# Letting transpositions and retention scores join TensorE's queue when their operands are estimated ready, in an fp32 two-block network

## The chip, the cores and the metric

One core of a Trainium2 chip runs the whole program once. The metric is the device time of one execution in microseconds; the time before is the median of three executions. A further execution was profiled, and every duration below comes from its trace.

## What is computed

256 tokens of width 2048 pass through two blocks, all in fp32 accuracy. Block 1 normalizes and modulates the tokens, mixes them, and runs a swiglu FFN of inner width 5632. Block 2 has its own mixer (attention, gated linear attention and a short convolution, merged by sigmoid gates) and a second FFN. What the change touches, cut from the reference:

```python
def token_mixer(h, ...):
    q, k, v, g_ret, u, gate_r, gate_s = jnp.split(h @ w_in, IN_SPLITS, axis=-1)
    q = rope(q, cos, sin)
    k = rope(k, cos, sin) * (RET_QK_DIM ** -0.5)
    ret = head_group_norm(retention(q, k, v))       # scores = q k^T * decay; 8 heads
    y_ret = (jax.nn.silu(g_ret) * ret) @ w_ret_out
    y_ssm = jax.nn.gelu(s5_ssm(u, ...))
    glu_a, glu_b = jnp.split(y_ssm @ w_s5_glu, 2, axis=-1)
    y_s5 = glu_a * jax.nn.sigmoid(glu_b)
    merged = jax.nn.sigmoid(gate_r) * y_ret + jax.nn.sigmoid(gate_s) * y_s5
    return merged @ w_out

def swiglu_ffn(h, w_ffn_in, w_ffn_out):
    a, b = jnp.split(h @ w_ffn_in, 2, axis=-1)
    return (jax.nn.silu(a) * b) @ w_ffn_out
```

## The kernel before

**Weights and items.** Every weight is used once. They come in units of 1 MB from `ws` into `raw` (four buffers, queue of SyncE). A unit holds two items of 128 rows x 1024 columns. For each item ScalarE copies `raw` into `whi` in a rounded format, VectorE subtracts to get `wlo`, and TensorE forms hi·hi, hi·lo and lo·hi: twelve matmuls of 128x512 per item (`gemm_tok`, `mm3`). Items are prepared up to four ahead (`AHEAD`, five buffers each of `whi` and `wlo`). Activations are kept as pairs of pages too (`h2h` and `h2l`, `ysh` and `ysl`, `xrh` and `xrl`). In between stand 96 modulation steps on VectorE, which multiply a whole `raw` by `cact`.

**Side tasks.** The rest is written as Python generators: `untok` (L446, turns token-major pages by TensorE transpositions against `ident` into a bank `sdb` and splits them), `retention` (L864), `gated` (L913), S5 and others. They yield the kind of engine that comes next and a delay: "P", "A", "V", or "W" for no condition. While the program is built, a planner keeps an estimated clock for each engine (`Engine`, `Times`). After each item `pump` steps the head task of each kind that `can` go on; "P" goes on if its time `t[2]` is no later than TensorE's clock plus `EARLY` = -0.25 us. For a new task, `t[2]` is that of its first yield:

```python
            t[3], wait = next(t[0])
            t[2] = max(self.times.mark, self.PE.clock if wait else 0.0) + wait
```

For `yield "P", 0.0` ahead of any instruction of the task itself, `mark` and `wait` are 0, so `t[2]` is 0: a task that starts with it goes on after the item that started it. `sd` yields "W" until one of three spare PSUM banks is estimated free. `finish` steps all tasks until a given one has ended. What is emitted is a fixed order on each engine; the planner does not exist on the chip.

**Who starts the tasks.** `gate_up` (FFN) multiplies the two banks of a stage into `fst` on VectorE and starts `untok` on them: 11 stages in each of two FFNs. `glu_a` multiplies the banks into `sg`, then by a gate page `gl`, adds `merged`, and starts `untok`: four times. `br_done` does the same with `sig` for the merge of block 2: four times. `ready` starts `retention(hp)` for a pair of heads when its q, k and v exist; q and k come from `rope_page` (two products and a sum on VectorE). `g_done(hp)` starts `gated(hp)`, which multiplies the retention output into `tg` and transposes it to `xr`, the input of the `w_ret_out` GEMM. Its four column groups of eight items each read `xr` through `xrf`; `ret_before(0)` first finishes all four `gated` tasks. S5 runs as a task beside all this, in four slabs of state; each fetches its inputs by many small DMAs and ends in the pages `ysh` and `ysl` of the glu stage.

All instructions show L150 in the profile, since `Engine` records each operation there; so they are told apart by the names of their tiles.

Of the kernel before, what the change touches and what calls it, by code (L numbers as in the profile page):

```python
# [24 lines left out]
EARLY = -0.25  # L25
# [128 lines left out]
class Core:  # L154
# [52 lines left out]
    def sd(self, n):  # L207
        while sum(self.times.free((f"bank{i}", 0)) <= self.PE.clock + BANK for i in self.sd_ids) < n:
            yield "W", 0.0
        self.sd_ids.sort(key=lambda i: self.times.free((f"bank{i}", 0)))  # L210
        return [self.sd_bank() for _ in range(n)]

    def sd_free(self, *banks):
        self.sd_ids.extend(self.sd_of.pop(b.tensor.name) for b in banks)
# [231 lines left out]
    def untok(self, pages, ident, dst, n, name):  # L446


        yield "P", 0.0
        for half in range(2):  # L450
            b, = yield from self.sd(1)
            for vb in range(2):
                for t in range(2):
                    at = 256 * half + 128 * vb
                    self.PE.transpose(b[:, 256 * vb + 128 * t:256 * vb + 128 * t + 128], pages[t][:, at:at + 128], ident)
            yield "A", 0.0
            dst[2 * n + half] = self.split_page(b, name)
            self.later.append(lambda b=b: self.sd_free(b))
            yield "P", 0.0
# [166 lines left out]
def program(K):  # L626
# [3 lines left out]
    G = {}  # L630
# [233 lines left out]
    def retention(hp):  # L864
        decs = [K.page("dec"), K.page("dec")]
        for par in range(2):
            K.S.dma_start(decs[par][:, :384], ins["decay"][:, 2 * hp + par, :])
        yield "P", 4.0
        q, k, v = qk["q", hp], qk["k", hp], vv.pop(hp)
        R = ret[hp] = [K.page("ret"), K.page("ret")]  # L870
        st = K.small.tile([128, 4, 6], F32, name="st", tag="st", bufs=2)
        mv = K.small.tile([128, 4, 2], F32, name="mv", tag="mv", bufs=2)
        rs = K.small.tile([128, 4], F32, name="rs", tag="rs", bufs=2)
        outs = []
        for par in range(2):
            rows = slice(64 * par, 64 * par + 64)
            dec = decs[par]
            s, = yield from K.sd(1)
            for j, i0, o0 in ((0, 0, 0), (1, 128, 256)):
                for half in range(2):  # L880
                    b = 256 * half
                    PE.matmul(s[:, o0:o0 + 256 - i0], k[rows, b + 128 * j:b + 128 * j + 128], q[rows, b + i0:b + 256],
                              start=half == 0, stop=half == 1)
            yield "V", 0.0
            sp = K.page("sp")
            V.tensor_mul(sp[:, :384], s[:, :384], dec[:, :384])
            K.sd_free(s)
            yield "P", 0.0
            o, = yield from K.sd(1)
            vs = slice(256 * par, 256 * par + 256)  # L890
            PE.matmul(o[:, :256], sp[:, 0:128], v[0][:, vs], start=True, stop=True)
            PE.matmul(o[:, 256:], sp[:, 128:256], v[0][:, vs], start=True, stop=False)
            PE.matmul(o[:, 256:], sp[:, 256:384], v[1][:, vs], start=False, stop=True)
            yield "V", 0.0
            for t in range(2):
                V.bn_stats(st[:, 2 * par + t, :], o[:, 256 * t:256 * t + 256])
                V.bn_aggr(mv[:, 2 * par + t, :], st[:, 2 * par + t, :])
            outs.append(o)
            yield "A", 0.0
        A.activation(rs, mv[:, :, 1], AF.Sqrt, bias=K.eps5)  # L900
        yield "V", 0.0
        V.reciprocal(rs, rs)
        for par in range(2):
            for t in range(2):
                n = 2 * par + t
                V.tensor_scalar(R[t][:, 256 * par:256 * par + 256], outs[par][:, 256 * t:256 * t + 256],
                                mv[:, n, 0:1], rs[:, n:n + 1], op0=OP.subtract, op1=OP.mult)
            yield "V", 0.0
        K.sd_free(*outs)

    xr = {}

    def gated(hp, tg):  # L913
        R = ret.pop(hp)
        for t in range(2):
            V.tensor_mul(tg[t], tg[t], R[t])
        yield "P", 0.0
        for par in range(2):
            b, = yield from K.sd(1)
            for vb in range(2):  # L920
                for t in range(2):
                    PE.transpose(b[:, 256 * vb + 128 * t:256 * vb + 128 * t + 128],
                                 tg[t][:, 256 * par + 128 * vb:256 * par + 128 * vb + 128], ident)
            yield "A", 0.0
            xr[2 * hp + par] = K.split_page(b, "xr")
            K.later.append(lambda b=b: K.sd_free(b))
            yield "P", 0.0
# [210 lines left out]
    def ready(it, src):  # L1138

        what, i = it  # L1140
        if what == "u":
            t = K.page("up")
            ut = t.rearrange("p (n t c) -> p n t c", n=2, t=4)
            uc = src[0].rearrange("p (n c t) -> p n t c", n=2, t=4)
            for n in range(2):
                A.activation(ut[:, n], uc[:, n], AF.Copy)
                K.G.dma_start(ub[2 * i + n], t[:, 256 * n:256 * n + 256])
        elif what == "v":
            vv[i] = [K.page("v"), K.page("v")]
            for p, ps in zip(vv[i], src):  # L1150
                A.activation(p, ps, AF.Copy)
        elif what in "rs":
            gate_done("rs".index(what), i)(0, src)
        else:
            qk[it] = rope_page(src[0], "qk")
        have.add(it)
        if what == "u" and all(("u", n) in have for n in range(4)):
            G["s5"] = K.start("s5", s5_run())
        for hp in range(4):
            if ("ret", hp) not in G and all((w, hp) in have for w in "qkv"):  # L1160
                G["ret", hp] = K.start("ret", retention(hp))
# [131 lines left out]
    def gate_load(n):  # L1293
        if n < 16 and n not in gl:
            gl[n] = K.page("gl")
            K.S.dma_start(gl[n], gsp[n])

    def ret_before(n):
        def f():
            if n == 0:  # L1300
                for hp in range(4):
                    K.finish(G["gt", hp])
                gate_load(0)
                gate_load(1)
            gate_load(2 * n + 2)
            gate_load(2 * n + 3)
        return f

    def ret_done(n):
# [2 lines left out]
                m = merged[n, t] = gl.pop(2 * n + t)  # L1312
                V.tensor_mul(m, ps, m)
        return f
    xrf = lambda k: K.halves_of(xr)(k)
    for n in range(4):
        K.gemm_tok([("w_ret_out", 512 * n)], xrf, ret_done(n), before=ret_before(n))

# [597 lines left out]
def plan():  # L1916
    K = Core()
    program(K)
    K.run()
    return K.units  # L1920
# [79 lines left out]
def trace(ctx, tc, ins, out, lives=None):  # L2000
    K = Core(tc, ins, out, ctx, lives)
    ctx.enter_context(tc.manual_schedule())
    program(K)
    K.run()
    return K
# [23 lines left out]
```

## Time and profile before

| | |
|---|---|
| median of three executions | 3358.95 us (3358.52 to 3359.52) |
| profiled execution | 3354.24 us, its span 3352.1 us |
| TensorE matmul (PE) busy | 3289.2 us, 98% |
| TensorE weight load (PEld) | 2773.6 us, 83% |
| VectorE (DVE) | 1994.5 us, 59% |
| ScalarE (ACT) | 1541.8 us, 46% |
| DMA | 737.62 MB, mean 220 GB/s |

Busy time is a share of the span. Matmuls are pipelined and their ends are modelled, so consecutive matmuls overlap in the rows; the distance between two starts is measured. The time that a row of the timeline has in brackets is the idle time of its engine ahead of it, with what released it. `PEclk` is the TensorE clock that was granted, as a share of full speed.

### The profile page before, as it was taken

Reading aid. Unit: us, or ns where it says so; the run is one execution under the profiler, and the core shown is the slowest. Engines: PE = TensorE matmul, PEld = TensorE weight load, DVE = VectorE, ACT = ScalarE, POOL = GpSimd, SP = SyncE. Lnnn points to the kernel's source line nnn. Section 1 sums busy time; section 2 is a strip of 40 time slices with the busy share of each in tenths; the row PEclk is TensorE's granted clock in tenths of the full one; section 3 lists DMA queues with packets and bytes.
Section 4 is the critical chain, followed back from the end, with each engine's and each line's share of the span. In section 5 each row is a group of like instructions: output and inputs, shape, how many; then the busy total and the mean of one; then the engine's idle time right before and its main releaser. Section 6 shows DMA issues by size and latency. Waiting matters only on the chain.

```text
span 3352.1 us, 42924 instructions
## 1 busy us (share of the span) xinstructions
PE 3289.2 (98%) x17276; PEld 2773.6 (83%) x17276; DVE 1994.5 (59%) x2192; ACT 1541.8 (46%) x1852; POOL 196.8 (6%) x311
## 2 busy tenths in 40 slices
PE   8999999999999999999999999999999999999999
PEld 7988888777888888888888999888778888888887
DVE  7987889777755565445545455455554544444444
ACT  5555555434644444444455444444434544444443
POOL 4611321100000000000000000000000000000000
PEclk9999999999999999999999999999999999999999
DMA  9976778777666666555555444555456455555653
GB/s 342 339 290 249 252 287 270 284 282 275 265 222 224 226 237 213 211 209 198 210 189 182 168 181 168 206 188 196 181 180 222 177 187 188 182 184 187 221 202 129
DMA packets 120489, 737.62 MB, mean 220 GB/s; under 512 B 15633, under 2 KB 19233, under 8 KB 36193
## 3 DMA queue, kind: packets, MB, share of 16 engines
q1 hardware_dynamic: 111778, 719.33, 59.1%
q0 software_dynamic: 7936, 14.50, 1.4%
q8 instruction: 135, 2.21, 0.3%
q10 hardware_dynamic: 576, 1.05, 0.1%
q14 instruction: 64, 0.52, 0.0%
HBM read 719.47 MB, written 14.70 MB: 219 GB/s over the span
## 4 chain that ended last, share of the span: by engine, by line
PE 89%; DVE 5%; DMA 3%; ACT 1%; issue 1%; SPq 0%; DVEq 0%; ACTq 0%
PE mmb L150 85%; PE sdb L150 4%; DMA raw<-ws 2%; DVE raw L150 1%; DVE wlo L150 1%; DVE fst L150 1%; ACT whi L150 1%; DVE sg L150 0%; ACT part L150 0%; DVE part L150 0%; DMA s5b<-s5bc 0%; DVE sig L150 0%; DVE t L150 0%; DVE u L150 0%; DVE xl L150 0%
## 5 line engine op out<-in xcount | busy, mean ns | idle before, releaser
L150 DVE TENSOR_TENSOR wlo<-raw,whi 128x1024 fp32r<-128x1024 f32 x1124 | 1365.6, 1224 | 1035.7 <-ACT whi L150 1034.4
L150 ACT ACTIVATE whi<-raw 128x1024 fp32r<-128x1024 f32 x1124 | 1183.7, 1059 | 1521.7 <-PE mmb L150 1355.8
L150 PE MATMUL mmb<-whi,hh 128*128 128x512 f32 x1169 | 463.1, 396 | 8.8 <-ACT part L150 4.5
L150 PE MATMUL mmb<-wlo,hh 128*128 128x512 f32 x1169 | 457.7, 392 | 2.8 <-DVE wlo L150 2.8
L150 PE MATMUL mmb<-whi,hl 128*128 128x512 f32 x1169 | 457.2, 391 | 0.0
L150 PE MATMUL mmb<-whi,h2h 128*128 128x512 f32 x704 | 276.5, 393 | 0.7 <-ACT h2h L150 0.7
L150 PE MATMUL mmb<-whi,h4h 128*128 128x512 f32 x704 | 276.5, 393 | 0.1
L150 PE MATMUL mmb<-whi,h4l 128*128 128x512 f32 x704 | 274.1, 389 | 0.4 <-DVE h4l L150 0.4
L150 PE MATMUL mmb<-wlo,h4h 128*128 128x512 f32 x704 | 274.3, 390 | 0.0
L150 PE MATMUL mmb<-wlo,h2h 128*128 128x512 f32 x704 | 274.3, 390 | 0.0
L150 PE MATMUL mmb<-whi,h2l 128*128 128x512 f32 x704 | 274.2, 389 | 0.0
L150 PEld LDWEIGHTS mmb<-whi,hh 128*128 128x128 f32 x1169 | 220.6, 189 | 56.7 <-ACT part L150 5.2
L150 PEld LDWEIGHTS mmb<-wlo,hh 128*128 128x128 f32 x1169 | 220.6, 189 | 51.5 <-DVE wlo L150 5.2
L150 PEld LDWEIGHTS mmb<-whi,hl 128*128 128x128 f32 x1169 | 220.7, 189 | 44.4
L150 DVE SCALAR_TENSOR_TENSOR raw<-raw,cact 128x2048 f32<-128x2048 f32 x96 | 219.5, 2286 | 17.2 <-DMA raw<-ws 16.7
L150 PE MATMUL mmb<-whi,h3h 128*128 128x512 f32 x576 | 227.5, 395 | 0.0
L150 PE MATMUL mmb<-whi,h3l 128*128 128x512 f32 x576 | 225.6, 392 | 0.0
L150 PE MATMUL mmb<-wlo,h3h 128*128 128x512 f32 x576 | 225.6, 392 | 0.0
L150 PE MATMUL mmb<-h3h,whi 128*128 128x256 f32 x784 | 225.4, 287 | 0.1
L150 PE MATMUL mmb<-h3l,whi 128*128 128x256 f32 x784 | 221.9, 283 | 0.6 <-DVE h3l L150 0.6
L150 PE MATMUL mmb<-h3h,wlo 128*128 128x256 f32 x784 | 221.8, 283 | 0.0
L150 PEld LDWEIGHTS mmb<-wlo,h4h 128*128 128x128 f32 x704 | 132.1, 188 | 27.8
(332 smaller groups left out, 4784.7 us busy)
## 6 DMA issues: line engine op xcount, KB each, us to landing
raw<-ws SPq DMA_DIRECT2D x657, 1024.0 KB, 4.9
gsp<-gate POOLq DMA_DIRECT2D x16, 256.0 KB, 6.3
gl<-gsp SPq DMA_DIRECT2D x16, 256.0 KB, 7.4
xl<-x1d SPq DMA_DIRECT2D x16, 256.0 KB, 5.3
x<-xT SPq DMA_DIRECT2D x8, 256.0 KB, 5.6
xl<-xt SPq DMA_DIRECT2D x8, 256.0 KB, 8.7
gb<-grow SPq DMA_DIRECT2D x8, 256.0 KB, 6.5
x1d<-u POOLq DMA_DIRECT2D x8, 256.0 KB, 3.5
```

The source lines that it names most:

```text
L150: return f(*args, **kw)
```

## The change

A new method `made` yields "W" for as long as the planner estimates that the operands named are not ready by TensorE's clock plus `EARLY`. `untok` calls it on its pages ahead of its first transposition, `retention` on q, k and the decay pages ahead of its first scores. `ret_before(0)` no longer finishes the gated tasks; `xrf(k)` finishes one when its pages are asked for and missing.

```diff
+    def made(self, *aps):
+        while self.PE.clock + EARLY < self.times.start(0.0, "", [], aps):
+            yield "W", 0.0
...
         yield "P", 0.0
+        yield from self.made(*pages)
         for half in range(2):
...
         yield "P", 4.0
         q, k, v = qk["q", hp], qk["k", hp], vv.pop(hp)
+        yield from K.made(q, k, decs[0], decs[1])
...
             if n == 0:
-                for hp in range(4):
-                    K.finish(G["gt", hp])
                 gate_load(0)
                 gate_load(1)
...
-    xrf = lambda k: K.halves_of(xr)(k)
+    def xrf(k):
+        if k // 2 not in xr:
+            K.finish(G["gt", k // 4])
+        return K.halves_of(xr)(k)
```

All engines have the same instructions as before, in another order. On TensorE, at the end of an FFN stage of block 1 (`mmb` are accumulators, `fst` the gated pages of that stage, `h2h` and `h2l` the FFN's input), before:

```order
L150 MATMUL mmb_8088<-whi_8354,h2h_8360 128x512
L150 MATMUL mmb_8088<-whi_8354,h2l_8361 128x512
L150 MATMUL mmb_8088<-wlo_8355,h2h_8360 128x512
L150 MATMUL sdb_8461<-ident_92,fst_8455 128x128
L150 MATMUL sdb_8461<-ident_92,fst_8456 128x128
...
L150 MATMUL mmb_8476<-whi_8385,h2h_8035 128x512
```

and with the change:

```order
L150 MATMUL mmb_8088<-wlo_8355,h2h_8360 128x512
L150 MATMUL mmb_8471<-whi_8385,h2h_8035 128x512
L150 MATMUL mmb_8471<-whi_8385,h2l_8036 128x512
L150 MATMUL mmb_8471<-wlo_8386,h2h_8035 128x512
L150 MATMUL mmb_8472<-whi_8385,h2h_8035 128x512
L150 MATMUL mmb_8472<-whi_8385,h2l_8036 128x512
L150 MATMUL mmb_8472<-wlo_8386,h2h_8035 128x512
...
L150 MATMUL sdb_8485<-ident_92,fst_8455 128x128
L150 MATMUL sdb_8485<-ident_92,fst_8456 128x128
...
L150 MATMUL mmb_8471<-whi_8405,h2h_8056 128x512
```

The first group of four transpositions stands one item (twelve matmuls, of which six are shown) further back, behind the first item of the next stage. The `sig` group moves in the same way, by one item.

On TensorE, at the end of a glu column group (`ysh` and `ysl` are the S5 output, `sg` the merged page), before:

```order
L150 MATMUL mmb_6681<-whi_6654,ysh_6378 128x512
L150 MATMUL mmb_6681<-whi_6654,ysl_6379 128x512
L150 MATMUL mmb_6681<-wlo_6655,ysh_6378 128x512
L150 MATMUL sdb_6754<-ident_92,sg_6670 128x128
L150 MATMUL sdb_6754<-ident_92,sg_6671 128x128
...
L150 MATMUL mmb_6769<-whi_6674,ysh_4077 128x512
```

and with the change:

```order
L150 MATMUL mmb_6681<-wlo_6655,ysh_6260 128x512
L150 MATMUL mmb_6764<-whi_6674,ysh_4131 128x512
...
L150 MATMUL mmb_6764<-whi_6694,ysh_4944 128x512
...
L150 MATMUL mmb_6765<-wlo_6695,ysh_4944 128x512
L150 MATMUL sdb_6794<-ident_92,sg_6670 128x128
L150 MATMUL sdb_6794<-ident_92,sg_6671 128x128
...
L150 MATMUL mmb_6764<-whi_6717,ysh_5629 128x512
```

Here two items (`whi_6674` and `whi_6694`, 24 matmuls) now stand between the last matmul of the group and its transpositions.

On TensorE, ahead of the `w_ret_out` GEMM (`tg` is the gated retention output, `u4` and `m1r` are S5's, `xrh` is the GEMM's input), before:

```order
L150 MATMUL mmb_5581<-wlo_5654,hh_1986 128x512
L150 MATMUL sdb_5834<-ident_92,tg_5811 128x128
L150 MATMUL sdb_5834<-ident_92,tg_5812 128x128
...
L150 MATMUL sdb_5845<-u4_5084,m1r_5488 64x64 x16
L150 MATMUL sdb_5846<-u4_5084,m1i_5489 64x64 x16
L150 MATMUL sdb_5879<-ident_92,tg_5811 128x128
L150 MATMUL sdb_5879<-ident_92,tg_5812 128x128
...
L150 MATMUL mmb_5900<-whi_5673,xrh_5166 128x512
```

and with the change:

```order
L150 MATMUL mmb_5895<-whi_5787,xrh_5176 128x512
...
L150 MATMUL sdb_5949<-u4_5043,m3_5510 64x64
L150 MATMUL sdb_5998<-ident_92,tg_5873 128x128
L150 MATMUL sdb_5998<-ident_92,tg_5874 128x128
...
L150 MATMUL mmb_5895<-whi_5857,xrh_5512 128x512
...
L150 MATMUL sdb_6042<-ident_92,tg_5873 128x128
L150 MATMUL sdb_6042<-ident_92,tg_5874 128x128
...
L150 MATMUL mmb_5895<-whi_5884,xrh_5760 128x512
```

The two groups of the last head pair stand behind the third and fourth item of the GEMM, not ahead of it, and no S5 products are placed between them by force. The first retention scores move back by 30 matmuls, into the first column group of a gate GEMM.

## Rows read from the trace of the kernel before

**Rows 1.** Waits of TensorE: who waits <- for whom: us in total, times, longest

```profile
PE sdb L150 <- DVE sg L150: 12.5, 8, 2.2
PE sdb L150 <- DVE fst L150: 9.2, 24, 0.8
PE sdb L150 <- DVE sig L150: 6.7, 8, 1.5
...
PE sdb L150 <- DVE qk L150: 2.7, 1, 2.7
PE sdb L150 <- DVE xrl L150: 2.4, 1, 2.4
PE sdb L150 <- DVE tg L150: 1.7, 2, 1.5
```

**Rows 2.** Timeline, TensorE and VectorE in FFN stages: start, us, engine, instruction

```profile
945.05 0.39 PE L150 MATMUL mmb<-wlo,h2h 128*128 128x512 f32 x1
...
947.18 0.48 PE L150 MATMUL mmb<-whi,h2h 128*128 128x512 f32 x1
...
1036.18 1.37 DVE L150 TENSOR_TENSOR fst<-mmb,fst 128x512 f32<-128x512 f32 x2 [2.67 <-PE mmb L150]
...
1036.43 0.39 PE L150 MATMUL mmb<-wlo,h2h 128*128 128x512 f32 x1
...
1037.91 0.48 PE L150 MATMUL mmb<-whi,h2h 128*128 128x512 f32 x1
...
1040.52 0.40 PE L150 MATMUL mmb<-wlo,h2h 128*128 128x512 f32 x1
...
1041.11 0.48 PE L150 MATMUL mmb<-whi,h2h 128*128 128x512 f32 x1
```

**Rows 3.** Timeline at the end of a glu column group, TensorE and VectorE

```profile
713.03 0.39 PE L150 MATMUL mmb<-wlo,ysh 128*128 128x512 f32 x1
...
714.07 2.74 DVE L150 TENSOR_TENSOR sg<-sg,gl 128x512 f32<-128x512 f32 x4
...
717.16 0.48 PE L150 MATMUL mmb<-whi,ysh 128*128 128x512 f32 x1
```

**Rows 4.** Timeline at the end of a merge column group of block 2, TensorE

```profile
2392.51 0.39 PE L150 MATMUL mmb<-wlo,xah 128*128 128x512 f32 x1
...
2395.19 0.48 PE L150 MATMUL mmb<-whi,h3h 128*128 128x512 f32 x1
```

**Rows 5.** Windows: us, busy PE PEld DVE ACT POOL, PEclk, DMA share, GB/s

```profile
294.90:298.40 3.50, 3.50 (x10) 2.69 (x10) 3.47 (x5) 0.00 (x0) 0.00 (x0) 0.51 0.52 176
...
2469.10:2472.60 3.50, 3.50 (x10) 2.61 (x10) 1.57 (x2) 0.25 (x1) 0.00 (x0) 0.51 0.69 250
500.00:520.00 20.00, 20.00 (x144) 16.55 (x143) 15.92 (x20) 11.02 (x13) 8.67 (x18) 1.00 0.86 158
680.00:700.00 20.00, 20.00 (x90) 16.57 (x89) 15.82 (x17) 7.69 (x8) 0.00 (x0) 1.00 0.99 385
700.00:820.00 120.00, 107.48 (x457) 86.89 (x456) 82.79 (x93) 46.70 (x52) 0.00 (x0) 0.94 0.70 255
```

**Rows 6.** Timeline around the first retention scores, TensorE and VectorE

```profile
288.71 1.29 DVE L150 TENSOR_TENSOR t<-s5x,s5b 128x512 f32<-128x512 f32 x2 [4.91 <-DMA s5b<-s5bc]
...
290.10 0.28 PE L150 MATMUL mmb<-hh,wlo 128*128 128x256 f32 x1
...
294.12 1.28 DVE L150 TENSOR_TENSOR rt<-mmb,rope 128x512 f32<-128x512 f32 x2
```

**Rows 7.** Timeline (ScalarE, TensorE) and one piece of the chain of waits

```profile
825.81 2.01 ACT L150 ACTIVATE whi<-raw 128x1024 fp32r<-128x1024 f32 x2 [8.47 <-DMA raw<-ws]
...
542.82 0.50 PE L150 MATMUL mmb<-wlo,hh 128*128 128x512 f32 x1 [0.58 <-DVE wlo L150]
...
506.66 15.99 DMA raw<-ws
```

**Rows 8.** Costliest groups of the page: busy us, mean ns | idle before

```profile
L150 DVE SCALAR_TENSOR_TENSOR raw<-raw,cact 128x2048 f32<-128x2048 f32 x96 | 219.5, 2286 | 17.2 <-DMA raw<-ws 16.7
```

## The prediction

> **What bounds the kernel now.** I read the table of the profile first: TensorE is busy 98% of a span of 3352.1 us, VectorE 59%, ScalarE 46%, so the end is set by TensorE's own list of matmuls and by what interrupts it. Next the waits of TensorE, grouped by who releases them [rows 1]. The reader should see that the named waits for `sg`, `fst`, `sig`, `qk`, `xrl` and `tg` are transpositions and retention scores (into the spare banks `sdb`) whose VectorE operands were still being made. They add up to 12.5 + 9.2 + 6.7 + 2.7 + 2.4 + 1.7 = 35.2 us. These are the places that the change edits.
>
> The ends of matmuls are modelled, so I take starts. In the FFN [rows 2] the last matmul of a stage starts at 1036.43 and the first of the next at 1037.91: 1.48 us, with four transpositions between them. One item later the same four transpositions, with their operands ready, fit between 1040.52 and 1041.11: 0.59 us. So a task's first group loses 1.48 - 0.59 = 0.89 us, its second nothing. The first task of each FFN takes 2.13 us (945.05 to 947.18) and loses 1.54. In the glu stage [rows 3] the first group spans 713.03 to 717.16: 4.13, a loss of 3.54. In the merge of block 2 [rows 4] 2392.51 to 2395.19: 2.68, a loss of 2.09.
>
> Last the granted clock by stretches [rows 5]: right after the wait for `qk`, each of the four for `sg` and two of the four for `sig`, TensorE is granted 0.51 for 3.5 us (seven such stretches; first and last stand there). That is the lower of its two levels, 1.2 instead of 2.4 GHz, nearly throughout, and loses 0.49 x 3.5 = 1.7 us each.
>
> **The change, part by part.** No instruction is added or removed on any engine; only their order differs. `made` costs nothing on the chip: it decides while the program is built. About ten DMA issues on SP's queue (decay and S5 loads among weights) and one group of S5 gathers on GpSimd's change places by a few; they are priced below with S5.
>
> *FFN transpositions.* There are 5632/512 = 11 tasks in each of two FFNs. Their first group goes behind one more item, twelve matmuls at 0.22 us (90 of them in 20.00 us, [rows 5]), 2.7 us. Are the operands there by then? VectorE's two products end at 1036.18 + 1.37 = 1037.55 [rows 2]; the transpositions would now start at 1036.43 + 0.23 + 2.7 = 1039.4. Margin 1.8 us. Removed: 20 x 0.89 + 2 x 1.54 = 20.9 us. The pages made from them are read in the down-projection, after all tasks; the last one moves into its first items, long before its own columns are due. What is late next: the ScalarE copy and VectorE subtraction of the transposed page, one item later, with nobody waiting.
>
> *Glu transpositions.* Four tasks go behind two items, 5.4 us. The last operand is made at 714.07 + 2.74 = 716.81 [rows 3]; the transpositions would start at 713.03 + 0.23 + 5.4 = 718.7. Margin 1.9 us. Removed: 4 x 3.54 = 14.2 us.
>
> *Merge transpositions (`sig`).* Four tasks go behind one item. After the present wait the next matmul starts at 2395.19 [rows 4], so operands are there before that; the new start is 2392.51 + 0.23 + 2.7 = 2395.4. Margin 0.2 us or more, the smallest. Removed: 4 x 2.09 = 8.4 us.
>
> *First retention scores.* 30 matmuls later. The wait is 2.7 us [rows 1]. Its cause stays: VectorE stands 4.91 us until 288.71 for the S5 parameters [rows 6], and three pairs of rope products queue up behind. Behind the scores stand the first items of a gate GEMM. TensorE's last matmul ahead starts at 290.10; 21 matmuls later, about 295.0, it wants a bank that the rope pair of 294.12 + 1.28 = 295.40 still reads. So about 0.4 us of a new wait; ends: nothing, or all of 2.7 + 1.7 = 4.4 given back.
>
> *Gated retention on demand.* The transpositions of the last head pair (`tg`, with `xrl` as the profile's other name for that wait) no longer stand ahead of the `ret_out` GEMM; they go behind its third and fourth item, and are due in the seventh. S5's chunk that was forced out with them spreads over the items. Removed 1.7 + 2.4 = 4.1 us [rows 1].
>
> *Half clock.* With their waits go the seven stretches: 7 x 1.7 = 11.9 us.
>
> Removed together: 20.9 + 14.2 + 8.4 + 2.7 + 4.1 + 11.9 = 62.2 us.
>
> **What is given back.** First the 0.4 us above. Second, weights: at the start of `w_out` eight 256 KB pages and gain rows share the queue, and ScalarE waits 8.47 us for `raw` [rows 7] while TensorE waits for nothing: four prepared items (4 x 2.7 = 10.8 us) cover it, with 2.4 to spare. The last glu task now brings TensorE there 3.5 + 1.7 = 5.2 us sooner: 5.2 - 2.4 = 2.8 us. Ends: 0 and 8.5. Third, S5 and retention are rearranged between 280 and 600, where VectorE is nearly full; I take two waits like the one of 0.58 us for a weight's low part [rows 7], 1 us; ends 0 and 3 (five of them). Sum 4.2 us, at the ends 0 and 15.9.
>
> Net: 62.2 - 4.2 = 58.0 us. The profiled execution took 3354.24 us, so I expect 3296.2 in a profile. The median shown, 3358.95, stands 4.7 above it, and 3358.95 - 58.0 = **3301.0 us**.
>
> **A rule weighed against the rows.** Starts in [rows 2 to 4] show 43.5 us for `fst`, `sg` and `sig`, idle time in [rows 1] 28.4. The Trainium skill, Perfetto Trace Analysis, "Tensor Engine Instruction (MATMUL, LD_WEIGHTS)", says that the profiler estimates a TensorE instruction's end, so that a wait can be partly hidden under the drawn end of the matmul ahead; the trace agrees (a 0.39 us matmul followed by another 0.22 us later). By idle time alone the sum would be 35.2 + 11.9 - 4.2 = 42.9 and the median 3316. I go by starts, since only they are measured.
>
> **The rivals.**
> 1. *Weights pace the stretch from 290 to 820 us*, so what is saved there turns into waits of `whi` for `raw`. Lost: 2.7 + 4.1 + 14.2 and five half-clock stretches (8.5), 29.5 us; left 20.9 + 8.4 + 3.4 = 32.7, time 3326.3. For it: 8.47 us in [rows 7]. Against it: DMA moves 255 GB/s at 0.70 share in 700 to 820 and would move 255 x 120/99 = 309 with the 14.2 us and four half-clock stretches (6.8) gone, where 385 at 0.99 has just been seen [rows 5].
> 2. *The change does not do what it says* at the short distances: readiness is the planner's estimate, and where VectorE runs behind it by one modulation step of 2286 ns [rows 8] the transposition still waits, an item later. The margins of 0.2 (`sig`) and 1.9 us (`sg`) are under that. If `sg` and `sig` keep waits and half clock: 14.2 + 8.4 + 6 x 1.7 = 32.8 lost, 25.2 left, time 3333.8. Against it: VectorE's order ahead of these products does not change, and the longest single waits (1.5 for `sig`, 2.2 for `sg`, 0.8 for `fst`, [rows 1]) are well under the 2.7 and 5.4 us by which the transpositions move, so no repetition was much later than the one shown.
> 3. *Slower: S5's fetches starve the weights.* S5's four slabs run between other items than before, the last one earlier, and their small gathers fall on other moments. The chain of waits of 480 to 620 has one DMA piece of 15.99 us on `raw` [rows 7], and in 500 to 520 the DMA engines are 0.86 busy for only 158 GB/s [rows 5]. Today TensorE feels only 0.58 us of it. Were each of four slabs to cost its 16 us and a half-clock stretch, 4 x 17.7 = 70.8 us would be lost against 58.0 gained: 12.8 slower, 3371.8. It decides from 58.0/4 = 14.5 us per slab. Against it: prepared items cover nearly all of it now, and slabs after the change are as many, in the same order. The Trainium skill, DMA: Bandwidth & Descriptors, "Specifications", says that transfers under 512 B do not reach line rate; S5's rows of 256 B agree with the 158 GB/s, and this speaks against any change that would bunch them.
>
> **How the numbers follow.** The forecast has 0.84; rival 1 0.05, rival 2 0.04, rival 3 0.04. A gain that is given back to within 0.2% (6.7 us, about what a measurement of this kernel can tell from no change) needs a large part of rival 3, or several rivals at once: 0.03. So faster 0.84 + 0.05 + 0.04 = 0.93, same 0.03, slower 0.04. The forecast's own ends are 3358.95 - 62.2 = 3296.8 and 3358.95 - 46.3 = 3312.7; 3 us below for the distance between one execution and a median, and some way up towards rivals 1 and 2, which start at 3326, give 3294 to 3320. That leaves out the rivals and the no-change case, 0.16, and a little of the forecast.
>
> **What would show it.** Right: no TensorE wait for `fst`, `sg`, `sig` and `tg` over 0.1 us each time; first groups of transpositions between starts 0.6 us apart; granted clock 1.0 from 700 to 820 and from 2380 to 2510; a wait under 1 us near 295 us; a profile span near 3294. Rival 1 shows as TensorE waiting for `whi` or `wlo` with ScalarE waiting for `raw`, between 290 and 820. Rival 2 shows as waits for `sg` or `sig` an item later, with their half-clock stretches. Rival 3 shows as DMA waits of TensorE of more than 10 us between 450 and 620. I am wrong if the gain is under 46 us with none of these waits in the trace: then it would be time between starts that no wait of before explains.

## The result and the profile after

| | before | with the change |
|---|---|---|
| first measurement, median | 3359.23 us (3358.52 to 3359.64, 4 executions) | 3297.02 us (3296.72 to 3299.26, 4) |
| ratio | | 0.9822, 95% interval 0.9809 to 0.9836 |
| second measurement, another job, median | 3354.43 us (3352.54 to 3358.03, 15) | 3299.16 us (3297.01 to 3300.07, 4) |
| ratio | | 0.9833, interval 0.982 to 0.9846 |
| profiled execution, span | 3352.1 us | 3295.4 us |

The forecast was 3301.0 us, in a range from 3294 to 3320. In medians the change gains 62.2 us the first time and 55.3 the second; between the profiled executions it gains 57.0 (3354.24 to 3297.21). The gain forecast was 58.0.

TensorE's waits in the changed kernel, to be read against [rows 1] (who waits <- for whom: us in total, times, longest), and whole:

```profile
PE mmb L150 <- DVE wlo L150: 5.5, 4, 3.9
PE mmb L150 <- ACT whi L150: 4.2, 2, 3.3
PE mmb L150 <- ACT part L150: 3.5, 1, 3.5
PE sdb L150 <- DVE sq L150: 3.0, 1, 3.0
PE mmb L150 <- ACT mmb L150: 1.8, 2, 1.2
PE mmb L150 <- DVE ones L150: 1.2, 1, 1.2
PE mmb L150 <- ACT h2h L150: 0.7, 1, 0.7
PE mmb L150 <- DVE h3l L150: 0.6, 1, 0.6
PE mmb L150 <- DVE h4l L150: 0.4, 1, 0.4
```

All six groups of [rows 1] are gone. `sq`, `part`, `ones` and `whi` belong to the first 100 us; they were there before, in about the same size together (11.9 us, before 11.5). New are a wait of 3.9 us for `wlo` and one of 0.6 us in the row of `mmb`; both are taken up below.

The timeline of TensorE at the three kinds of transposition, to be read against [rows 2 to 4]: the last matmul ahead, the four transpositions, the first matmul behind.

```profile
707.46 0.39 PE L150 MATMUL mmb<-wlo,ysh 128*128 128x512 f32 x1
707.69 0.60 PE L150 MATMUL sdb<-ident,sg 128*128 128x128 f32 x4
708.04 0.48 PE L150 MATMUL mmb<-whi,ysh 128*128 128x512 f32 x1
...
1012.19 0.39 PE L150 MATMUL mmb<-wlo,h2h 128*128 128x512 f32 x1
1012.42 0.60 PE L150 MATMUL sdb<-ident,fst 128*128 128x128 f32 x4
1012.77 0.48 PE L150 MATMUL mmb<-whi,h2h 128*128 128x512 f32 x1
...
2360.34 0.39 PE L150 MATMUL mmb<-wlo,h3h 128*128 128x512 f32 x1
2360.57 0.60 PE L150 MATMUL sdb<-ident,sig 128*128 128x128 f32 x4
2360.93 0.48 PE L150 MATMUL mmb<-whi,h3h 128*128 128x512 f32 x1
```

The first group of `sg` takes 0.58 us from start to start (707.46 to 708.04) where it took 4.13, that of `fst` 0.58 where it took 1.48, that of `sig` 0.59 where it took 2.68. No row has a bracket: the engine waited for nothing.

Windows of the changed kernel (columns as in [rows 5]):

```profile
700.00:820.00 120.00, 116.12 (x516) 95.54 (x515) 95.93 (x111) 51.97 (x63) 0.00 (x0) 0.97 0.80 304
799.10:805.90 6.80, 5.53 (x13) 4.37 (x14) 6.50 (x11) 6.38 (x12) 0.00 (x0) 0.50 0.86 329
2350.00:2480.00 130.00, 130.00 (x590) 107.59 (x589) 70.41 (x70) 56.67 (x61) 0.00 (x0) 1.00 0.55 205
```

DMA moves 304 GB/s from 700 to 820, where it moved 255; the forecast had 309. The granted clock is 1.00 through the merge. But it is 0.50 for 6.8 us from 799.1 on, that is, from inside the new wait; TensorE works in 5.53 us of this stretch and waits in the other 1.27. The timeline of VectorE and TensorE there, and below it that of SyncE's queue, show what that wait is:

```profile
796.62 2.29 DVE L150 SCALAR_TENSOR_TENSOR raw<-raw,cact 128x2048 f32<-128x2048 f32 x1 [9.71 <-DMA raw<-ws]
...
800.37 0.80 PE L150 MATMUL mmb<-wlo,mgh 128*128 128x512 f32 x1 [3.88 <-DVE wlo L150]
```

```profile
779.62 5.05 SPq L131 DMA_DIRECT2D xl<-xt  x5
785.32 3.26 SPq L131 DMA_DIRECT2D gb<-grow  x4
788.92 16.93 SPq L131 DMA_DIRECT2D raw<-ws  x6
```

The second fence has start, us, and the transfers (of the eight `xl`, the five that fall into the stretch asked for). At the start of `w_out` pages `xl` and gain rows `gb` go ahead of the weights. The next `raw` lands near 796.6; VectorE waits 9.71 us for it, then does the modulation step that stands first, then `wlo`, and TensorE stands still from about 796.3 to 800.37.

**Where the time went, by stage.** From the starts of the first matmul of each stage in both traces (before, after), gains and what the prediction's terms say for that stage:

| stage | ends at, before | ends at, after | gain | by the prediction's terms |
|---|---|---|---|---|
| up to the glu GEMM | 691.50 | 680.48 | 11.0 | 2.7 + 1.7 + 4.1 - 0.4 - 1.0 = 7.1 |
| glu | 800.89 | 770.42 | 19.5 | 14.2 + 3 x 1.7 = 19.3 |
| `w_out`, norm | 898.47 | 873.92 | -5.9 | 1.7 - 2.8 = -1.1 |
| FFN of block 1, up | 1400.84 | 1365.59 | 10.7 | 10 x 0.89 + 1.54 = 10.4 |
| down, block 2 to the merge | 2381.86 | 2346.97 | -0.4 | 0 |
| merge | 2505.43 | 2458.67 | 11.9 | 8.4 + 2 x 1.7 = 11.8 |
| `w_out` of block 2 | 2597.97 | 2551.59 | -0.4 | 0 |
| FFN of block 2, up | 3100.79 | 3043.67 | 10.7 | 10.4 |
| to the end | 3352.1 | 3295.4 | -0.4 | 0 |

A group of transpositions adds 0.59 - 0.23 = 0.36 us to the stage in which it stands; the -0.4 of three stages are groups that moved into them across their boundary, and the stages ahead of these (both FFNs and the merge) show a gain that is too large by as much; the glu stage hands one group to `w_out` in the same way. The gains sum to 56.7 us, the terms to the 58.0 of the forecast, but for rounding. Two stages differ from their terms: the first gained 3.9 more, `w_out` gave back 4.8 more.

### The profile page after: what moved, and what is told of

It is laid out like the page before. It is cut to its first block, busy times and chain, and to the rows that moved or that the text cites. A ratio compares the mean times of both kernels' runs of the same rounds, so it can differ in the third digit from the quotient of the medians.

```text
span 3295.4 us, 42934 instructions
## 1 busy us (share of the span) xinstructions
PE 3266.3 (99%) x17276; PEld 2768.3 (84%) x17276; DVE 1993.7 (60%) x2192; ACT 1539.3 (47%) x1852; POOL 201.2 (6%) x311
## 4 chain that ended last, share of the span: by engine, by line
PE 94%; DVE 3%; DMA 1%; ACT 1%; issue 0%; SPq 0%; DVEq 0%; ACTq 0%
PE mmb L150 89%; PE sdb L150 5%; DMA raw<-ws 1%; DVE wlo L150 1%; DVE raw L150 1%; DMA s5b<-s5bc 0%; DMA xl<-xt 0%; DVE part L150 0%; DVE u L150 0%; ACT whi L150 0%; ACT part L150 0%; DVE xl L150 0%; DVE mt L150 0%; DVE junk L150 0%; DVE rt L150 0%
```

## The experiments

The theory is that of the prediction: waits of TensorE for its own transpositions, with the half clock behind them, are the gain, and weights at `w_out` the giveback. Each edit below is against the kernel before, if nothing else is said, and where it calls `made`, that method is added with it. "Before" stands for executions of the kernel before in the same job.

**FFN transpositions alone.**

```diff
+        if name == "h":
+            yield from self.made(*pages)
```

> The readiness test for the FFN transpositions alone (name "h"); the glu and merge transpositions, the retention scores and the forced finish of gated retention stay as before. Starts of matmuls: 20 tasks x 0.89 + 2 x 1.54 = 20.9 us gained, so 3359.2 - 20.9 = 3338.3. Rival, by the idle column alone: 9.2 us, 3350.0. If unprofiled executions of before also lose clock at the first FFN tasks (the median of before is 4.7 us above its profiled execution), some 2 to 5 us more than 20.9.

Measured: 3331.10 us (3330.41 to 3333.96) beside 3354.86 for before in the same job (3347.90 to 3366.43, 16 executions), ratio 0.9935 (0.9922 to 0.9949). By stages the trace has 10.7 us in each FFN, 21.4 together, or 20.7 without the group that each hands on to the next stage: the starts (20.9) are right, the idle column, that is, the idle time that [rows 1] sum up (9.2), is not. The median gains 23.8. In the trace, 3.2 us more come from the merge (120.4 us, before 123.6), and that is clock: in this execution no half clock followed the `sig` waits, which are the same 6.7 us as before. Windows over the merge, of before, of this kernel, and of the kernel with moved scores alone (below):

```profile
2380.00:2510.00 130.00, 123.32 (x539) 100.12 (x539) 65.91 (x66) 53.39 (x59) 0.00 (x0) 0.97 0.47 169
```

```profile
2380.00:2510.00 130.00, 123.32 (x554) 100.49 (x553) 67.16 (x68) 53.95 (x58) 0.00 (x0) 1.00 0.53 189
```

```profile
2380.00:2510.00 130.00, 123.32 (x530) 99.92 (x529) 65.26 (x65) 52.03 (x58) 0.00 (x0) 0.96 0.46 164
```

TensorE's busy time, and so its idle time, is the same in all three; the granted clock is 0.97, 1.00 and 0.96. These are single executions of three kernels that have the same order in this stage. So like waits were followed by half clock in one execution and not in another, and in the merge this moves the time by up to 5 us (three stretches or none). It may be one reason why executions of before lie up to 18 us apart; that it is the main one is not shown.

**Glu transpositions alone.** The same edit with `"mg"`.

> The readiness test for the glu transpositions alone (name "mg"). Removed by starts 14.2 us and four half-clock stretches 6.8, together 21.0. Theory: the new wait of the changed kernel at the start of w_out (3.9 us, then half clock for 6.8 us, 7.3 in all) is caused by arriving there sooner, which the glu part alone does by 21 us: net 13.7, 3345.5, with a TensorE wait for wlo near 807 us. Rival: the wait comes only when the earlier stretch has also been shortened (retention part): net 21.0, 3338.2, no such wait.

Measured: 3342.52 us (3340.02 to 3352.45), ratio 0.9966 (0.9954 to 0.9978). The glu stage gains 19.5 us in the trace (0.7 ahead before it, 20.1 behind), and 7.1 are lost again in `w_out`. The wait is there without any retention part:

```profile
PE mmb L150 <- DVE wlo L150: 7.0, 4, 5.4
```

and in the chain of waits (start, us, what) the loads stand ahead of the weights as in the change:

```profile
791.06 10.02 DMA xl<-xt
...
801.17 7.35 DMA raw<-ws
...
808.54 2.31 DVE raw L150 x2
...
811.01 1.23 DVE wlo L150
...
812.29 17.87 PE mmb L150 x68
```

By these two stages the net is 12.4 us, the median gains 12.3, and 13.7 were expected. So arriving at `w_out` sooner than its weights is the glu part's own giveback; the rival is out.

**Merge transpositions alone.** The same edit with `"mx"`.

> The readiness test for the merge transpositions of block 2 alone (name "mx"). Removed by starts 8.4 us, and two half-clock stretches, 3.4: 11.8, 3347.4. Rival, by the idle column and no clock: 6.7 us, 3352.5. If the two sig waits that kept the clock in the profiled execution lose it in others, up to 15.2 us, 3344.

Measured: 3343.27 us (3341.70 to 3347.39), ratio 0.9970 (0.9958 to 0.9981). The median gains 11.6 us, and the merge 11.9 in the trace, as expected against a profiled execution with two half-clock stretches there.

**Retention part alone** (scores and gated on demand).

> The readiness test for retention scores and gated retention on demand; all transpositions of untok as before. Forecast of the prediction: 2.7 + 1.7 + 4.1 - 0.4 - 1.0 = 7.1 us, 3352.1. By starts of the two traces from 280 to 692 us: 2.9 + 1.7 + 4.7 + 0.7 - 1.1 = 8.9, 3350.3. Rival: S5's rearrangement costs what the waits give: no change, 3359.

Measured: 3344.78 us (3343.44 to 3351.61), ratio 0.9975 (0.9964 to 0.9986). The median gains 10.1 us. In the trace the glu GEMM starts 7.4 us sooner than before; this execution had half clock for 6.8 us, not 3.4, at the first `sg` wait, so 6.1 are left at the end. But part of such a difference is older than the edit. TensorE's first 1700 matmuls are the same in all kernels here, in the same order, and the last of them starts anywhere from 288.45 to 292.65 us (before 290.10, here 292.11). Counted from there to the glu GEMM, the five traces with the old order take 399.7 to 403.6 us (before 401.4), the five with the whole retention part 391.2 to 392.0 (here 392.0). So the part gains 9.4 us: more than the forecast's 7.1, near the 8.9 by starts; the rival (no change) is out.

**Its two halves.** First the scores alone, with the forced finish of the gated tasks ahead of the `w_ret_out` GEMM kept:

```diff
         q, k, v = qk["q", hp], qk["k", hp], vv.pop(hp)
+        yield from K.made(q, k, decs[0], decs[1])
```

> The readiness test for the first retention scores alone; gated retention finished by force and all transpositions as before. The wait for qk (2.1 to 2.9 us by starts in the traces so far) goes, with the half clock after it (1.7), against 0.8 us of the new bank wait near 293: 3 to 4 us at 600 us of the trace. The two waits for tg and xrl stay (4.7 by starts). Rival: the scores' later place is what removed the wait for a weight's low part near 542 and S5's, and gains 1 to 2 us more.

Measured: 3356.83 us (3350.89 to 3359.04) beside 3355.28 (3352.11 to 3358.60, 19 executions), ratio 1.0003 (0.9993 to 1.0012): nothing is gained, which neither expectation had. The wait for `qk` is gone, and so is that near 542; but the forced finish now waits longer for `tg`. TensorE, first in the kernel before, then in this one:

```profile
593.22 0.39 PE L150 MATMUL mmb<-wlo,hh 128*128 128x512 f32 x1
595.10 0.30 PE L150 MATMUL sdb<-ident,tg 128*128 128x128 f32 x1 [1.49 <-DVE tg L150]
```

```profile
589.37 0.39 PE L150 MATMUL mmb<-wlo,hh 128*128 128x512 f32 x1
594.89 1.50 PE L150 MATMUL sdb<-ident,tg 128*128 128x128 f32 x4 [5.13 <-DVE tg L150]
```

VectorE makes these `tg` pages at the same time in both, from 594.15 us on here and from 594.27 before. TensorE only comes to them 3.9 us sooner, and stands. The window from the last 1.3 us of this wait on:

```profile
593.60:603.60 10.00, 8.20 (x105) 7.30 (x105) 7.82 (x11) 2.48 (x3) 0.00 (x0) 0.50 0.88 307
```

What the scores gained is spent in this one wait, of 5.13 us, and in ten microseconds at half clock. Counted from the last common matmul the glu GEMM comes after 401.3 us, before after 401.4.

Then gated retention on demand alone:

> Gated retention on demand alone; retention scores and all transpositions as before. The waits for tg and xrl go, 4.7 us by starts, with a half-clock stretch in executions that had one there; the wait for qk stays. 4 to 6 us at the start of the glu stage. Rival: without the moved scores S5's forced chunk is late in another place, and nothing is gained.

Measured: 3351.23 us (3345.82 to 3355.05), ratio 0.9988 (0.9978 to 0.9997), 4.1 us less, as expected; TensorE still waits 2.1 us for `qk`. From the last common matmul to the glu GEMM the trace takes 396.3 us, 5.1 less than before. So on-demand gating gains alone, the scores only together with it: apart the two have 0.1 + 5.1 = 5.2 us in this stretch, both at once 9.4. Each of the halves has one trace, and the traces with the old order lie up to 3.8 us apart, so the sizes are rough; the medians (nothing, 4.1 and 10.1 us) say the same.

**The change again, and with its loads spread.** The edit is against the change:

```diff
-        if n == 0:
-            reload("xl", xsrc)
-            for i in range(4):
-                load_rows(2, i)
+        for t in range(2):
+            load_x("xl", xsrc, 2 * n + t)
+        load_rows(2, n)
```

> The changed kernel itself, beside the others of this job. 58 us less than before in a profiled execution as forecast, or 62 as in the first measurement; executions of before differ by up to 18 us among themselves, those of the change should differ by less, since seven waits that can be followed by half clock are gone. Wait of TensorE for wlo of about 4 us near 797, with half clock after it.

> The change, and at w_out the eight pages xl and the four gain rows are loaded with the column group that uses them, 0.75 MB ahead of each group, not 3 MB ahead of the first. Theory: the wait near 797 us comes from the weights queued behind these loads; it goes, with its 6.8 us of half clock: 3.9 + 3.4 = 7.3 us faster than the change. Rival: total bytes per time set the pace from 700 to 820, the weights arrive as late as now: no difference, the wait moves by some us.

Measured on the same chip: 3299.16 us (3297.01 to 3300.07) for the change, 3290.78 (3290.08 to 3291.79) with spread loads, ratios to before 0.9833 (0.982 to 0.9846) and 0.9809 (0.9796 to 0.9823). That is 8.4 us less. The four executions of the change lie 3.1 us apart, the 15 of before 5.5. From the first matmul of `w_out` to the first of the FFN the trace with spread loads takes 96.7 us (770.03 to 866.76), that of the change in the same job 104.0 (771.03 to 875.02): the 7.3 expected, though in this execution 5.0 of them are the wait and about 2.3 half clock. Another 1.0 us lies ahead of `w_out`, where the edit changes nothing. A window of the version with spread loads:

```profile
700.00:820.00 120.00, 120.00 (x546) 99.29 (x545) 101.50 (x120) 56.13 (x73) 0.00 (x0) 1.00 0.80 304
```

TensorE is busy without a gap and at full clock through glu and `w_out`, at the same 304 GB/s: it was the order in the queue, not the bytes per time; the rival is out. This version beats both kernels.

**Spread loads in the kernel before.** The same edit.

> The same spreading of loads in the kernel before. There the prepared items cover ScalarE's 8.47 us for raw and TensorE does not wait: no change in the time (within 2 us in a profiled execution, half-clock stretches apart). Rival: loads in one burst cost TensorE time in before as well, 3 us or more faster.

Measured: 3354.94 us (3349.39 to 3359.32) beside 3354.43, ratio 0.9999 (0.9989 to 1.0008): no difference, as expected. The burst cost nothing as long as TensorE came later.

**The transpositions one item sooner** (against the change, `made` with a slack of one item for `untok`):

```diff
-    def made(self, *aps):
+    def made(self, *aps, slack=0.0):
...
-        while self.PE.clock + EARLY < self.times.start(0.0, "", [], aps):
+        while self.PE.clock + EARLY + slack < self.times.start(0.0, "", [], aps):
...
-        yield from self.made(*pages)
+        yield from self.made(*pages, slack=2.72)
```

> The change with the test for transpositions passed one item (2.72 us of the planner's clock) sooner: FFN and merge transpositions stand where before had them, the glu ones one item back, the rest as in the change. By the rows of before: fst waits back (20.9 us), sig waits back (8.4, and up to 3.4 of half clock), sg ready at 716.81 against a start at 713.03 + 0.23 + 2.7 = 715.96: 0.9 us for each of four, 3.4, perhaps with half clock. Sum 33 to 43 us slower than the change, less some of the giveback at w_out. Rival: one item is enough for sg as well (VectorE's products end sooner when TensorE is not held up): 29 to 33.

Measured: 3330.50 us (3329.75 to 3334.78), ratio to before 0.9930 (0.9916 to 0.9943), 31.3 us above the change. The waits:

```profile
PE sdb L150 <- DVE fst L150: 9.2, 24, 0.8
PE sdb L150 <- DVE sig L150: 6.7, 8, 1.5
...
PE sdb L150 <- DVE sg L150: 2.5, 4, 0.7
```

`fst` and `sig` have their old waits. For `sg` one item is nearly enough: 0.6 to 0.7 us in each of four (2.5 in all), with no half clock of their own. 20.9 + 8.4 + 2.5 = 31.8 us; one stretch of half clock behind the first `sig` wait makes it 33.5, against 32.0 between the two profiled executions (3330.43 and 3298.38). The measured 31.3 lies in the rival's range (29 to 33), not in that of the expectation (33 to 43), which had 0.9 us for each `sg`.

## Why the prediction was right

**Transpositions: right, in size too.** With their half clock, and without the 0.36 us of each group that moved into the next stage, the FFNs gained 20.7 us for 20.9, the glu stage 19.1 for 19.3, the merge 11.5 for 11.8. Going by starts carried this; with the idle column the forecast would have been 3316, 19 us too high. The margins held: the smallest, `sig`, has no wait in any repetition, and one item for `sg` falls short by 0.6 us where [rows 3] gave 716.81 - 715.96 = 0.9.

**The sum: closer than its terms.** That 57.0 us were measured for 58.0 is partly luck: the stage up to the glu GEMM gained 3.9 us more than its terms, `w_out` gave back 4.8 more, and the two nearly cancel.

**Half clock: right for the execution that was profiled.** Its seven stretches went. But which waits are followed by one, and for how long, changes between executions: the four `sig` waits had none, one, two or three in different traces. The forecast counted none for the forced finish of gated retention, as the trace before has none there; the four other traces that keep this finish in the old order (FFN, glu and merge alone, spread loads before) have 3.4 or 6.8 us of half clock at its waits, so in other executions the change removes more than was counted. That the medians gain 62.2 one time and 55.3 another, with 57.0 between the profiled executions, lies mostly in before: its medians were 3359.23, 3354.86, 3354.43 and 3355.28 in four measurements, those of the change 3297.02 and 3299.16.

**Given back at `w_out`: right place, too small.** The term was 5.2 us of earlier arrival less 2.4 of cover, 2.8 us. The new wait costs 4.0 between starts (796.10 to 800.37 less a normal 0.23), and the step left out the half clock that came with it: TensorE worked in 5.53 us of those 6.8 us at 0.50, which loses 2.8. Together 6.8, within the bound of 8.5, and as much as `w_out` is longer than with spread loads (103.5 and 96.7 us). So one sign that was named, a granted clock of 1.0 from 700 to 820, did not come: it was 0.97.

**S5 and retention: too small, and one term with the wrong sign.** The retention part gained 9.4 us, not 7.1. S5's rearrangement was taken as 1.0 us of new waits; TensorE's timeline has no wait between 320 and 600 us, and the 0.58 us of [rows 7] is gone too. The bank wait near 293 came as described, at 0.6 and 0.1 us idle, about 1.0 between starts for the 0.4 of the forecast:

```profile
294.58 0.50 PE L150 MATMUL mmb<-whi,hh 128*128 128x512 f32 x1 [0.60 <-ACT mmb L150]
```

```profile
293.92 0.60 ACT L150 ACTIVATE mmb<-part 128x512 f32<-128x512 f32 x1 [0.97 <-DVE rt L150]
```

It is ScalarE that releases it: the bank is filled with earlier partial sums, and that copy waits for the rope pair; the forecast had left the copy out. `tg` and `xrl` are 4.7 us by starts (593.22 to 596.09 and the wait at 600.60), not the 4.1 that I took from the idle column against my own rule. About 1.6 us of the first stage's gain is no effect of the change: it is there by 288.50, where TensorE's last matmul ahead of the moved scores starts, at 290.10 before [rows 6], and up to there the order is the same. Most of it is a wait of 1.15 us for `wlo` near 202 us, which the profiled execution of before has and that of the change has not.

**The rivals.** Weights do not pace the stretch from 290 to 820; they are late at one point, and there because of the order in one queue (spread loads). The change does what it says: no wait for `sg`, `sig`, `fst` or `tg` is left. S5's fetches cost TensorE nothing in that stretch. Whether S5's small rows cause the 158 GB/s of [rows 5] stays open: of the 0.86 share, 0.16 is their queue and 0.70 is the queue of the large loads, which moved 2.9 of the 3.2 MB. What I had not listed is that a part of the change could need another: the scores alone gain nothing.

What stays open: whether half clock follows a given wait in a given execution. The traces show that it differs, not what decides it.

## What to carry to other kernels

Work that is queued in order on the bounding engine should stand where its operands are ready, even if its results are needed only later; one item's distance (2.7 us) was enough where a group took 1.5 or 2.7 us between starts, two where it took 4.1. Price such waits between starts, not by the idle column, and look at the granted clock behind each. Where a half-clock stretch begins inside a wait, price only the part in which the engine works. When the bounding engine speeds up, look for the next burst of loads ahead of its weights: here it took back 7 of 20 us until the loads were spread, and cost nothing before. When two profiles are compared, count from the last instruction that both have in the same order; here the two starts differed by 1.6 us ahead of any change.

## What the runs showed that was not expected

Time that one task gains can be lost again at the next forced finish: with the scores alone moved, VectorE made `tg` no sooner, so TensorE's wait ahead of the `w_ret_out` GEMM grew to 5.13 us, with 10 us at half clock around its end. And three kernels with the same order and the same waits to 0.1 us in the merge stage were granted 1.00, 0.97 and 0.96 of the clock there, one execution each. That different executions of one kernel differ in the same way is likely but not shown; the profiled execution of before stands 4.7 us under its median.
